# Splitting projection weights once instead of five times, and re-timing loads, operand splits and the last norm of an encoder-trunk kernel

## The chip, the core and the metric

The kernel runs on one core of a Trainium2 chip. The metric is the device time of one execution in microseconds (us), as a median of runs. The engines are named as in the profile: PE multiplies matrices, PEld loads PE's stationary operand beside it, DVE, ACT and POOL work elementwise, SP only issues DMA transfers, and 16 DMA engines carry them.

## What is computed

One layer on 2,304 tokens (2,048 of one sequence, 256 of another) of width 1,024, all in fp32: a norm, an input projection, three token mixers, an output projection with a residual, a norm, a gated feed-forward part with a width-3 convolution, a residual, and a last norm.

```python
h = rmsnorm(x, norm1_g)
q, k, v, g, lr, u, vs, xp = jnp.split(h @ w_in, IN_SPLITS, axis=-1)
a_out = gla_mixer(q, k, v, g, lr, gla_gate_w2, gla_gate_b, gla_norm_g)
b_out = spatial_gating(gelu(u), gelu(vs), sgu_ln_g, sgu_ln_b, sgu_w, sgu_b)
c_out = pool_mixer(xp, pool_w, pool_scale)
x = x + jnp.concatenate([a_out, b_out, c_out], axis=-1) @ w_o
a, up = jnp.split(rmsnorm(x, norm2_g) @ w_ffn_in, 2, axis=-1)
x = x + (silu(conv3(a)) * up) @ w_ffn_out
y = rmsnorm(x, norm_f)
```

## The kernel before, in words

**Products.** Every large product is made in a split form. `split` writes a high part of an fp32 operand (a copy on ACT into a rounded type) and a low part (a subtraction on DVE, or on POOL where it is asked to), and `mm3` multiplies high by high, high by low and low by high into one PSUM bank. So an operand costs one ACT and one DVE or POOL instruction before PE can use it.

**Stages.** A first sweep over 18 tiles of 128 tokens makes the attention part and prepares, beside it, the output projection's weights: `wo_prep(c)` loads column block c of eight, scales it, folds the pooling weights in and stores it to DRAM as `d_w[c]`. A second sweep goes over the tiles in five groups (`SUPERS`, of 3, 4, 3, 4 and 4 tiles); after each group `out2` multiplies its mixed tokens with all eight column blocks and adds the residual. The feed-forward part then goes over three blocks of 768 tokens, each as two halves q = 0 and 1. Per block, `ffn1` runs 22 times (j = 0 to 21): seven products of four steps, in a form with sums of operands (A and S are weight operands, B and T token operands). After every two or three of these, `ffn2` multiplies the result with eight column blocks of the second weight and adds it into `x2`. `finish` makes the last norm of a half, and `last_norm` that of the very last half.

**Order of the work.** PE's order is the order of the code. Beside it runs a `Pipe`: generators that issue a few instructions, then give a number of ticks to wait. `pipe.tick()` stands behind each step of three matmuls (about 0.53 us in the feed-forward part), so a number in a `yield` or in `pipe.add(gen, delay)` places elementwise work and DMAs beside a step of PE. From the second tile of the second sweep on, DVE, ACT, POOL and SP also keep the order of the code; in the first sweep a planner orders them. An instruction that waits holds all behind it on its engine, SP's DMAs too.

**Names that the change touches.** `wo_load` and `wo_split` load a half of `d_w[c]` (256 KB) and split it, in each of the five groups again; `ahead2` does the first ones before `out2` begins, and `look(u)` says how many column blocks ahead the loads go (2 in the last group, else 3). `xr_load` fetches the residual. `stat2` closes `out2`: short matmuls with one column each sum the squares. `load2f` fetches a half of `x2` (four DMAs for both halves); for the first block both are issued right after `out2`, ahead of the first `ffn1`. `bload` fetches the next block's token operands (16 pieces: four for each of four slices kk; pieces p = 0, 1, 2 hold two operands, p = 3 one) and splits them, from tick 30 of the block's last `ffn1` on, one piece each three ticks, in the order p = 0, 2, 1, 3; p = 1 and 3 have their low parts on POOL, p = 0 and 2 on DVE. It has one buffer per p, so a piece waits until PE has used the old one. `gate` makes the result of `ffn1`; the last gates of a block stand around ticks 21 to 31 of j = 21. In the last part `sqadd` squares each column of `x2` on ACT (two buffers) and adds it up on POOL. `prepw2` splits a piece of the second weight (`gh` on ACT, `gl` on DVE) six ticks before PE uses it.

In the tail, the rest of half 1's `finish` (products on DVE and output DMAs) is issued by `pipe.flush()` before `last_norm` begins:

```python
if final:
    pipe.flush()
    last_norm(blk, 0, xs, no, accs[0][0])
```

Of the kernel before, what the change touches and what calls it, by code (L numbers as in the profile page):

```python
# [10 lines left out]
F32 = mybir.dt.float32  # L11
# [7 lines left out]
P = 128  # L19
# [33 lines left out]
HL = (1, 2)  # L53
# [34 lines left out]
EARLY = 2  # L88
NAMES = ("A11", "S1", "S2", "S3", "S4", "A12", "A22")
# [31 lines left out]
def trunk(ctx: ExitStack, tc: tile.TileContext, xT, wa, wb, gw2, gb, rows, wsT, plw, wo, w1, w2, vec, cst, yT):  # L121
# [14 lines left out]
    def rawt(name):  # L136
        return rawp.tile([P, 1024], F32, tag="raw", name=name)
# [5 lines left out]
    d_w = [dr.tile([P, KD, P], F32, name=f"dw{c}") for c in range(KD)]  # L143
# [46 lines left out]
    if True:  # L190
# [273 lines left out]
        def wo_prep(c):  # L464
# [11 lines left out]
            GP.dma_start(out=d_w[c], in_=rv)  # L476
# [19 lines left out]
    if True:  # L496
# [163 lines left out]
        def wo_load(u, c, a):  # L660
            if u == len(SUPERS) - 1:
                rv = box2["acc"].tile([P, 4, P], F32, tag="wr", name="wr", bufs=4)
            else:
                if a == 0:
                    wx["raw", c] = rawt("rawo").rearrange("p (k n) -> p k n", k=KD)
                rv = wx["raw", c][:, 4 * a:4 * a + 4]
            wx["raw", c, a] = rv
            SY.dma_start(out=rv, in_=d_w[c][:, 4 * a:4 * a + 4])

        def wo_split(c, a):  # L670
            if a == 0:
                wx["h"] = box2["o"].tile([P, KD, P], F32R, tag="oh", name="oh")
                wx["l"] = box2["o"].tile([P, KD, P], F32R, tag="ol", name="ol")
            split(wx["h"][:, 4 * a:4 * a + 4], wx["l"][:, 4 * a:4 * a + 4], wx.pop(("raw", c, a)))
# [63 lines left out]
        def look(u):  # L738
            return 2 if u == len(SUPERS) - 1 else 3

        def ahead2(u):

            for c in range(look(u)):
                for a in range(2):
                    wo_load(u, c, a)
            wx[0] = xr_load(u, 0)
            yield 8
            for a in range(2):
                wo_split(0, a)
                wo_load(u, look(u), a)  # L750
                yield 2

        def out2(u, get, between=None, begun=None):
# [15 lines left out]
            for c in range(KD):  # L769
                oh, ol, xr = wx.pop("h"), wx.pop("l"), wx.pop(c)  # L770
                pw_ = pmt("pw") if c or not begun else begun
                for k in range(KD):
                    if c or not begun or k < 4:
                        mm3(pw_[:, 0:n], oh[:, k], ol[:, k], mh[:, k, 0:n], ml[:, k, 0:n], k == 0 and (c > 0 or not begun),
                            k == (3 if begun and not c else KD - 1))
# [92 lines left out]
    if True:  # L868
# [144 lines left out]
        def bload(bi, box):  # L1013
# [8 lines left out]

            for p, _ in PAIRS:
                load(0, p)
# [436 lines left out]
```

## Time and profile before

| what | value |
|---|---|
| median of 3 runs (lowest to highest) | 2462.21 us (2461.95 to 2464.28) |
| the profiled execution's own time | 2461.97 us |
| its span, first to last instruction | 2460.2 us |
| busy: PE | 2396.1 us, 97% |
| busy: DVE / ACT / POOL | 1655.8 / 1035.6 / 793.2 us |
| mean clock granted to PE | 0.989 of full |
| DMA | 343.52 MB, 140 GB/s mean |

The span lies 1.8 us below the time of its execution. Busy shares are means over stages that differ, so the text reads single stages. A clock of 1.00 is the level of 2.4 GHz, 0.50 that of 1.2 GHz; a window's figure between them is a mean over both.

### The profile page before, as it was taken

What the parts mean: (1) busy time and instruction counts of PE and PEld (TensorE: products, weight loads), DVE (VectorE), ACT (ScalarE), POOL (GpSimd) and SP (SyncE); (2) the same over time, 40 slices, a digit from 0 to 9 for tenths busy, and PEclk for the clock granted to TensorE, in tenths of its full rate; (3) what the DMA queues carried; (4) which work ended last, traced back from release to release, by engine and by line L of the source; (5) the groups of instructions that cost most, each with busy time, mean ns of one, the idle gap of its engine ahead of it and who ended that gap; (6) DMA issues with size and microseconds to landing.
All of it is one profiled execution on the core that took longest, in us unless ns stands there. A gap on an engine that the chain in (4) does not pass through costs nothing.

```text
span 2460.2 us, 37106 instructions
## 1 busy us (share of the span) xinstructions
PE 2396.1 (97%) x13416; PEld 2282.8 (93%) x13416; DVE 1655.8 (67%) x2963; ACT 1035.6 (42%) x1928; POOL 793.2 (32%) x748
## 2 busy tenths in 40 slices
PE   8999998999999989999999999999999999999997
PEld 7999997988988789999999899999999999999997
DVE  6755557676666876777867786666676665666666
ACT  6444444333332443433434544433344533444334
POOL 3332221010011664455545622323224521222122
PEclk9999999999999999999999999999999999999998
DMA  6333224555663653445434563444434543333232
GB/s 201 136 129 111 78 73 133 175 184 150 212 195 117 206 189 109 154 160 163 161 112 134 167 223 117 142 135 127 127 101 156 175 140 100 103 112 104 90 95 87
DMA packets 227772, 343.52 MB, mean 140 GB/s; under 512 B 25634, under 2 KB 124962, under 8 KB 227588
## 3 DMA queue, kind: packets, MB, share of 16 engines
q1 hardware_dynamic: 220564, 318.21, 41.2%
q0 software_dynamic: 6752, 22.55, 2.4%
q8 instruction: 106, 1.74, 0.3%
q14 instruction: 78, 0.64, 0.1%
q10 hardware_dynamic: 272, 0.39, 0.0%
HBM read 261.81 MB, written 79.25 MB: 139 GB/s over the span
## 4 chain that ended last, share of the span: by engine, by line
PE 52%; DVE 5%; issue 3%; POOL 3%; DMA 1%; ACT 1%; SPq 0%; DVEq 0%; POOLq 0%; ACTq 0%
PE py L172 7%; PE py L171 6%; PE py L170 6%; PE fA L1142 3%; PE fD L1140 3%; PE fA L1140 3%; PE fA L1141 3%; PE fD L1141 3%; PE fD L1142 3%; PE fB L1140 2%; PE fB L1142 2%; PE fB L1141 2%; PE fC L1140 2%; PE fC L1142 2%; PE fC L1141 2%
## 5 line engine op out<-in xcount | busy, mean ns | idle before, releaser
L163 POOL TENSOR_TENSOR S<-S,S 128x512 fp32r<-128x512 f32 x242 | 329.8, 1363 | 756.0 <-ACT S L162 719.3
L172 PE MATMUL py<-uh,gl 128*128 128x384 f32 (+1 forms) x1056 | 359.5, 340 | 6.3 <-DVE gl L1207 6.1
L170 PE MATMUL py<-uh,gh 128*128 128x384 f32 (+1 forms) x1056 | 359.8, 341 | 5.5 <-ACT gh L1205 5.4
L171 PE MATMUL py<-ul,gh 128*128 128x384 f32 (+1 forms) x1056 | 358.8, 340 | 3.8 <-DVE ul L1170 3.8
L1252 DVE TENSOR_TENSOR x<-py,x 128x384 f32<-128x384 f32 (+1 forms) x384 | 212.9, 556 | 159.4 <-PE py L172 157.5
L163 DVE TENSOR_TENSOR A<-A,A 128x512 fp32r<-128x512 f32 x198 | 157.0, 793 | 176.4 <-ACT A L162 167.9
L162 ACT ACTIVATE A<-A 128x512 fp32r<-128x512 f32 x198 | 124.4, 630 | 215.8 <-issue 71.3
L172 PEld LDWEIGHTS py<-uh,gl 128*128 128x128 f32 x1056 | 200.2, 190 | 10.0 <-DVE gl L1207 9.9
L162 ACT ACTIVATE S<-S 128x512 fp32r<-128x512 f32 x242 | 152.2, 629 | 135.3 <-PE fE L1142 63.9
L170 PEld LDWEIGHTS py<-uh,gh 128*128 128x128 f32 x1056 | 200.2, 190 | 7.8 <-ACT gh L1205 7.0
L171 PEld LDWEIGHTS py<-ul,gh 128*128 128x128 f32 x1056 | 200.0, 189 | 5.7 <-DVE ul L1170 5.3
L1205 ACT ACTIVATE gh<-rg 128x384 fp32r<-128x384 f32 (+1 forms) x198 | 97.3, 493 | 223.9 <-PE py L171 207.2
L1140 PE MATMUL fA<-B,A 128*128 128x386 f32 (+1 forms) x528 | 179.9, 341 | 0.0
L1142 PE MATMUL fA<-B,A 128*128 128x386 f32 (+1 forms) x528 | 179.1, 339 | 0.0
L1141 PE MATMUL fA<-B,A 128*128 128x386 f32 (+1 forms) x528 | 178.4, 338 | 0.0
L170 PE MATMUL pm<-wk,xh 128*128 128x512 f32 (+2 forms) x432 | 166.4, 385 | 7.3 <-ACT wk L165 7.3
L172 PE MATMUL pm<-wk,xl 128*128 128x512 f32 (+2 forms) x432 | 156.2, 362 | 1.3 <-DVE xl L163 1.3
L171 PE MATMUL pm<-wk,xh 128*128 128x512 f32 (+2 forms) x432 | 157.0, 363 | 0.1
L1207 DVE TENSOR_TENSOR gl<-rg,gh 128x384 fp32r<-128x384 f32 (+1 forms) x198 | 118.8, 600 | 11.6 <-ACT gh L1205 11.5
L170 PE MATMUL qm<-vk,xh 128*128 128x512 f32 x288 | 120.8, 420 | 2.0 <-ACT vk L165 2.0
L172 PE MATMUL pw<-mh,ol 128*128 128x512 f32 (+1 forms) x320 | 118.6, 371 | 3.0 <-DVE ol L163 3.0
L171 PE MATMUL pw<-ml,oh 128*128 128x512 f32 (+1 forms) x320 | 118.4, 370 | 0.0
(278 smaller groups left out, 6231.3 us busy)
## 6 DMA issues: line engine op xcount, KB each, us to landing
A<-in_w SPq DMA_DIRECT2D x242, 256.0 KB, 3.7
S<-ds_S SPq DMA_DIRECT2D x176, 256.0 KB, 2.7
rg<-in_w SPq DMA_DIRECT2D x150, 192.0 KB, 2.8
xt<-in_xT SPq DMA_DIRECT2D x35, 512.0 KB, 4.2
ds_S<-S SPq DMA_DIRECT2D x66, 256.0 KB, 2.3
rawo<-dw SPq DMA_DIRECT2D x64, 256.0 KB, 4.5
dx<-xr SPq DMA_DIRECT2D x24, 256.0 KB, 2.5
rg<-in_w SPq DMA_DIRECT2D x48, 128.0 KB, 2.4
```

The source lines that it names most:

```text
L162: SC.activation(hi, src, AF.Copy)
L163: (eng or V).tensor_tensor(out=lo, in0=src, in1=hi.bitcast(F32), op=ALU.subtract)
L170: TE.matmul(out, lh, rhs_h, start=first, stop=False)
L171: TE.matmul(out, lh, rhs_l, start=False, stop=False)
L172: TE.matmul(out, ll, rhs_h, start=False, stop=last)
L1140: TE.matmul(o, ah, bh, start=st, stop=False, skip_group_check=True)
L1141: TE.matmul(o, ah, bl, start=False, stop=False, skip_group_check=True)
L1142: TE.matmul(o, al, bh, start=False, stop=kk == 3, skip_group_check=True)
L1205: SC.activation(gh[:, 0:n], rv, AF.Copy)
L1207: V.tensor_tensor(out=gl[:, 0:n], in0=rv, in1=gh[:, 0:n].bitcast(F32), op=ALU.subtract)
L1252: V.tensor_tensor(out=x2[:, c, 1:1 + no], in0=py[q][:, 0:no], in1=x2[:, c, 1:1 + no], op=ALU.add)
```

## The change

The change has five parts, all in `trunk`. `wo_prep` splits its weights right after it has folded them and stores both parts (`d_w` becomes twice as large); `wo_load` fetches both parts of a half (512 KB) and `wo_split` is gone; all groups look three column blocks ahead, and the residual's first load goes ahead of the weights'. `bload` follows a written list `BORDER` of (kk, p, tick): the four pieces p = 2 at ticks 13 to 22 of the last `ffn1`, p = 0 and 1 at ticks 42 to 68, p = 3 at ticks 78 to 90; three loads go ahead instead of four. The first block's two `x2` loads are issued at ticks 30 and 60 of it. `stat2` after the last group comes at 16 ticks instead of 8, and `finish` of a non-final block starts at 14 and 36 ticks instead of 2 and 28. In the tail, `last_norm` is issued ahead of the rest of half 1's `finish`, which is flushed in its middle, and all its small diagonal pieces are made on ACT.

```diff
@@ -50,7 +50,9 @@
-HL = (1, 2)
+XG = 30
+BORDER = ((0, 2, 13), (1, 2, 16), (2, 2, 19), (3, 2, 22), (0, 0, 42), (0, 1, 45), (1, 0, 48), (1, 1, 52),
+          (2, 0, 56), (2, 1, 60), (3, 0, 64), (3, 1, 68), (0, 3, 78), (1, 3, 82), (2, 3, 86), (3, 3, 90))
@@ -86,6 +88,7 @@
+LOOK = 3
@@ -133,14 +136,14 @@
-    def rawt(name):
-        return rawp.tile([P, 1024], F32, tag="raw", name=name)
+    def rawt(name, dtype=F32):
+        return rawp.tile([P, 1024], dtype, tag="raw", name=name)
...
-    d_w = [dr.tile([P, KD, P], F32, name=f"dw{c}") for c in range(KD)]
+    d_w = [dr.tile([P, 2, KD, P], F32, name=f"dw{c}") for c in range(KD)]
@@ -473,7 +476,12 @@
             SC.activation(raw[:, 6 * P:8 * P], pf[:, 0:2 * P], AF.Copy)
-            GP.dma_start(out=d_w[c], in_=rv)
+            yield 2
+            hi = rawt("rawh", F32R)
+            split(hi, raw.bitcast(F32R), raw)
+            yield 3
+            GP.dma_start(out=d_w[c][:, 0], in_=hi.bitcast(F32).rearrange("p (k n) -> p k n", k=KD))
+            GP.dma_start(out=d_w[c][:, 1], in_=rv)
@@ -657,21 +665,9 @@
-        def wo_load(u, c, a):
-            if u == len(SUPERS) - 1:
-                rv = box2["acc"].tile([P, 4, P], F32, tag="wr", name="wr", bufs=4)
-            else:
-                if a == 0:
-                    wx["raw", c] = rawt("rawo").rearrange("p (k n) -> p k n", k=KD)
-                rv = wx["raw", c][:, 4 * a:4 * a + 4]
-            wx["raw", c, a] = rv
-            SY.dma_start(out=rv, in_=d_w[c][:, 4 * a:4 * a + 4])
-        def wo_split(c, a):
-            if a == 0:
-                wx["h"] = box2["o"].tile([P, KD, P], F32R, tag="oh", name="oh")
-                wx["l"] = box2["o"].tile([P, KD, P], F32R, tag="ol", name="ol")
-            split(wx["h"][:, 4 * a:4 * a + 4], wx["l"][:, 4 * a:4 * a + 4], wx.pop(("raw", c, a)))
+        def wo_load(c, a):
+            wx[c, a] = t = box2["o"].tile([P, 2, 4, P], F32R, tag="ow", name="ow", bufs=2 * LOOK)
+            SY.dma_start(out=t.bitcast(F32), in_=d_w[c][:, :, 4 * a:4 * a + 4])
@@ -735,20 +731,13 @@
-        def look(u):
-            return 2 if u == len(SUPERS) - 1 else 3
         def ahead2(u):
...
-            for c in range(look(u)):
+            wx[0] = xr_load(u, 0)
+            for c in range(LOOK):
...
-                    wo_load(u, c, a)
-            wx[0] = xr_load(u, 0)
-            yield 8
-            for a in range(2):
-                wo_split(0, a)
-                wo_load(u, look(u), a)
-                yield 2
+                    wo_load(c, a)
+                yield 1
...
         def out2(u, get, between=None, begun=None):
@@ -767,16 +756,16 @@
-                oh, ol, xr = wx.pop("h"), wx.pop("l"), wx.pop(c)
+                ow, xr = [wx.pop((c, a)) for a in range(2)], wx.pop(c)
...
                 for k in range(KD):
...
-                        mm3(pw_[:, 0:n], oh[:, k], ol[:, k], mh[:, k, 0:n], ml[:, k, 0:n], k == 0 and (c > 0 or not begun),
-                            k == (3 if begun and not c else KD - 1))
-                    if c + 1 < KD and k in (0, 1):
-                        wo_split(c + 1, k)
-                    if c + 1 + look(u) < KD and k in (3, 5):
-                        wo_load(u, c + 1 + look(u), k // 2 - 1)
+                        mm3(pw_[:, 0:n], ow[k // 4][:, 0, k % 4], ow[k // 4][:, 1, k % 4], mh[:, k, 0:n], ml[:, k, 0:n],
+                            k == 0 and (c > 0 or not begun), k == (3 if begun and not c else KD - 1))
+                    if k == 5 and c + LOOK < KD:
+                        wo_load(c + LOOK, 0)
+                    if k == 1 and 0 < c <= KD - LOOK:
+                        wo_load(c + LOOK - 1, 1)
@@ -790,7 +779,7 @@
-            pipe.add(stat2(u, acc, alloc), 8)
+            pipe.add(stat2(u, acc, alloc), 16 if between else 8)
@@ -854,7 +843,7 @@
-            mm3(begun[:, 0:w], wx["h"][:, k], wx["l"][:, k], mh[:, k, 0:w], ml[:, k, 0:w], k == 6, False)
+            mm3(begun[:, 0:w], wx[0, 1][:, 0, k % 4], wx[0, 1][:, 1, k % 4], mh[:, k, 0:w], ml[:, k, 0:w], k == 6, False)
@@ -924,7 +913,6 @@
-        PAIRS = ((0, V), (2, V), (1, GP), (3, GP))
@@ -1020,19 +1008,23 @@
-            for p, _ in PAIRS:
-                load(0, p)
-            yield box["wait"]
-            for kk in range(4):
-                for p, eng in PAIRS:
-                    m = 2 if p < 3 else 1
-                    hi, src = B[p][:, 0, 0:m, kk, 0:w], got.pop((kk, p))
-                    SC.activation(hi, src, AF.Copy)
-                    yield HL[0]
-                    eng.tensor_tensor(out=B[p][:, 1, 0:m, kk, 0:w], in0=src, in1=hi.bitcast(F32), op=ALU.subtract)
-                    yield HL[1]
-                    if kk < 3:
-                        load(kk + 1, p)
+            todo = [(kk, p) for kk, p, _ in BORDER]
+            for kk, p in todo[:NX - 1]:
+                load(kk, p)
+            at = 0
+            for n, (kk, p, tick) in enumerate(BORDER):
+                if tick > at:
+                    yield tick - at
+                    at = tick
+                m = 2 if p < 3 else 1
+                hi, src = B[p][:, 0, 0:m, kk, 0:w], got.pop((kk, p))
+                SC.activation(hi, src, AF.Copy)
+                yield 1
+                (GP if p % 2 else V).tensor_tensor(out=B[p][:, 1, 0:m, kk, 0:w], in0=src, in1=hi.bitcast(F32), op=ALU.subtract)
+                yield 1
+                at += 2
+                if n + NX - 1 < len(todo):
+                    load(*todo[n + NX - 1])
@@ -1319,11 +1311,8 @@
-                o, i, sc = dg[:, b * P:b * P + n], ident[:, P - n:P], r[:, b:b + 1]
-                if b % 2:
-                    SC.activation(o, i, AF.Copy, scale=sc)
-                else:
-                    V.tensor_scalar(out=o, in0=i, scalar1=sc, scalar2=None, op0=ALU.mult)
+                SC.activation(dg[:, b * P:b * P + n], ident[:, P - n:P], AF.Copy, scale=r[:, b:b + 1])
+            pipe.flush()
             TE.matmul(pr, ones, dg, start=True, stop=True)
@@ -1343,13 +1332,20 @@
-        xs = {q: load2f(segs, q, box["w"]) for q, segs in enumerate(BLOCKS[0])}
+        xs = {}
+        def first_x(w):
+            for q, segs in enumerate(BLOCKS[0]):
+                xs[q] = load2f(segs, q, w)
+                yield XG
+        pipe.add(first_x(box["w"]), XG)
...
-            nbox = {"wait": 30}
+            nbox = {}
@@ -1374,14 +1370,13 @@
             if final:
-                pipe.flush()
...
                         nx[q] = load2f(segs, q, w)
-                    pipe.add(finish(blk, q, xs, no, accs[q][0], FG, nxt), 2 + 26 * q)
+                    pipe.add(finish(blk, q, xs, no, accs[q][0], FG, nxt), 14 + 22 * q)
...
```

## Rows read from the trace of the kernel before

**Rows 1.** The page, section 1: busy time, share of the span, instructions.
```profile
PE 2396.1 (97%) x13416; PEld 2282.8 (93%) x13416; DVE 1655.8 (67%) x2963; ACT 1035.6 (42%) x1928; POOL 793.2 (32%) x748
```

**Rows 2.** The view of waits, PE alone: us in total, times, longest.
```profile
PE pw L172 <- DVE ol L163: 3.0, 3, 2.0
```

**Rows 3.** PE's timeline: start, us, instruction; in brackets the idle time before it.
```profile
854.40 1.19 PE L688 MATMUL pn<-ones,acc 128*128 128x1 f32 x8 [1.69 <-DVE acc L767]
...
871.66 0.66 PE L1140 MATMUL fD<-B,A 128*128 128x386 f32 x1 [6.11 <-DVE u L1149]
...
1364.31 0.44 PE L171 MATMUL py<-ul,gh 128*128 128x384 f32 x1 [2.06 <-DVE ul L1170]
...
1383.61 0.44 PE L170 MATMUL py<-uh,gh 128*128 128x384 f32 x1 [2.14 <-ACT gh L1205]
...
1384.98 0.69 PE L172 MATMUL py<-uh,gl 128*128 128x384 f32 x1 [0.76 <-DVE gl L1207]
...
1399.25 0.83 PE L1272 MATMUL pn<-ones,acc 128*128 128x1 f32 x6 [1.06 <-POOL acc L1226]
...
1907.92 0.44 PE L170 MATMUL py<-uh,gh 128*128 128x384 f32 x1 [2.13 <-ACT gh L1205]
...
1924.07 1.44 PE L1272 MATMUL pn<-ones,acc 128*128 128x1 f32 x6 [2.75 <-POOL acc L1226]
```

**Rows 4.** Windows behind six waits: us, busy (count) by engine, PEclk, DMA share, GB/s.
```profile
826.50:832.00 5.50, 5.12 (x15) 3.61 (x16) 5.50 (x7) 1.47 (x4) 3.11 (x3) 0.69 0.69 228
854.40:859.00 4.60, 4.60 (x20) 4.60 (x21) 0.77 (x2) 1.75 (x4) 3.56 (x3) 0.63 0.94 311
871.66:876.50 4.84, 4.84 (x17) 4.84 (x18) 3.15 (x4) 3.83 (x5) 4.76 (x4) 0.59 0.39 144
1383.60:1392.00 8.40, 7.64 (x26) 7.32 (x27) 6.41 (x8) 5.86 (x11) 8.40 (x7) 0.59 0.62 186
1907.90:1914.00 6.10, 5.33 (x20) 5.01 (x21) 4.46 (x7) 4.49 (x8) 6.10 (x5) 0.72 0.47 149
1924.07:1932.00 7.93, 7.93 (x31) 7.93 (x32) 1.88 (x4) 1.51 (x4) 2.94 (x3) 0.61 0.21 67
```

**Rows 5.** Groups by line, shapes kept apart: busy us, mean ns, idle before.
```profile
L1226 POOL TENSOR_TENSOR acc<-acc,sq 128x384 f32<-128x384 f32 x28 | 36.6, 1325 | 0.0
...
L163 DVE TENSOR_TENSOR ol<-wr,oh 128x512 fp32r<-128x512 f32 x16 | 13.4, 870 | 0.0
```

**Rows 6.** Windows of the two sweeps, columns as in rows 4.
```profile
123.00:369.00 246.00, 245.91 (x1573) 225.98 (x1572) 140.06 (x298) 116.92 (x219) 69.83 (x134) 1.00 0.27 98
441.00:848.00 407.00, 403.63 (x2032) 347.09 (x2031) 275.40 (x624) 145.63 (x285) 72.74 (x66) 1.00 0.58 179
614.30:654.30 40.00, 40.00 (x223) 38.39 (x222) 27.07 (x59) 16.85 (x35) 2.62 (x2) 1.00 0.72 234
799.50:848.00 48.50, 45.49 (x189) 35.50 (x189) 43.60 (x55) 24.57 (x54) 31.34 (x27) 0.96 0.71 218
```

**Rows 7.** SP's timeline behind the second sweep.
```profile
853.71 7.00 SPq L906 DMA_DIRECT2D x<-dx  x4
```

**Rows 8.** The chain that ended last, in that stretch: start, us, what.
```profile
861.45 8.15 DMA A<-in_w
```

**Rows 9.** Line 1032: duration in ns (min/median/max), first and last start.
```profile
L1032 DVE TENSOR_TENSOR B<-b,B x16: 952/1308/1598, 1365.1 to 1914.4; 128x772 fp32r<-128x772 f32 x8, 128x776 fp32r<-128x776 f32 x8
...
L1032 POOL TENSOR_TENSOR B<-b,B x16: 1012/1802/2182, 1367.9 to 1921.6; 128x772 fp32r<-128x772 f32 x4, 128x386 fp32r<-128x386 f32 x4, 128x776 fp32r<-128x776 f32 x4, 128x388 fp32r<-128x388 f32 x4
```

**Rows 10.** Windows of the last `ffn1` of blocks 0 and 1, columns as in rows 4.
```profile
1344.80:1359.50 14.70, 14.70 (x86) 14.70 (x85) 12.54 (x18) 7.95 (x15) 6.20 (x5) 1.00 0.99 333
1870.00:1884.80 14.80, 14.80 (x86) 14.80 (x85) 10.78 (x19) 7.83 (x16) 4.21 (x4) 1.00 0.75 257
```

**Rows 11.** DMA issues: count, KB each, median us to landing.
```profile
b<-db SPq DMA_DIRECT2D x12, 386.0 KB, 3.7
```

**Rows 12.** DVE's timeline in the tail.
```profile
2443.34 3.27 DVE L1289 SCALAR_TENSOR_TENSOR x<-x,vc,acc 128x386 f32<-128x386 f32 x6
```

## Prediction, made before the change was run

> **What bounds the kernel now.** I read the page first: PE is busy for 2396.1 us [rows 1], so of the 2460.2 us of span only 64 are to be had, and they stand where PE waits. The view of waits, filtered to PE, then says for whom, and PE's timeline says when: the reader is to look at the bracket at the end of each line, the idle time before it and its releaser. The waits come in four places. In the last group's `out2` (799 to 848 us) PE waits 3.0 us for `ol`, the low part of a projection weight [rows 2]. Just behind it come 1.69 us before `stat2`'s short matmuls and 6.11 us for a DVE addition [rows 3]. At the ends of blocks 0 and 1 come, in order, a wait for `ul` (2.06 us at the first end), a pair for `gh` and `gl` (2.14 and 0.76; the second end has the like, from 2.13) and one for POOL's `acc` (1.06 and 2.75) [rows 3]. Last comes the tail. Third, I looked at the granted clock right behind each wait, in windows that begin when PE resumes. It lies between 0.59 and 0.72 there [rows 4], so PE pays twice: the wait, and (1 - clock) of the window. That is 1.7, 1.7, 2.0, 3.4, 1.7 and 3.1 us, 13.6 in all.
>
> **The clock.** The rows say that a wait or a close pair of 2.9 us and more is followed by the low level, that 2.75 was too, and that 2.06 alone was not: PE ran at 1.00 after it. The 1.69 us fell together with eight one-column matmuls and was followed by 0.63 [rows 3, 4].
>
> **Weights split once.** Removed are 80 pairs of ACT and DVE instructions, 16 for each group; in the last group those on DVE take 870 ns each, 13.4 us [rows 5]. In the groups before PE has no wait (40.00 of 40.00 us busy in the third [rows 6]), so nothing is gained there. In the last one DVE is busy for 43.6 of 48.5 us [rows 6], the splits are most of 13.4 of these, and PE's wait for them goes: 3.0 us and the 1.7 of clock behind it, 4.7. The bounds are 0 (the same wait comes back for the weights' DMA) and 4.7; I take 4.7, because loads three of eight column blocks ahead have some 18 of these 48.5 us to land. The price is eight splits of twice the width and eight more stores in the first sweep. By twice the nearest row they are below 8 x 1.74 = 14 us of DVE, over a stretch in which DVE is busy 140 of 246 us and PE never waits [rows 6]: cover enough, so nothing. If that cover were gone, the 14 us would be paid. SP has two weight buffers instead of four to run ahead with, and the token loads queue behind it. Since these loads have the same sweep as cover, I put them at nothing too.
>
> The other price is traffic. Eighty loads grow by 256 KB, 21.0 MB. In the tightest group 234 GB/s took a share of 0.72, so a full share is 325 GB/s, and 21.0 MB are 64.5 us of transfer. From 441 to 848 us the DMA engines are free for 0.42 x 407 = 171 us [rows 6]. It is hidden if the loads can use that; in the tightest group 11.2 us are free in 40 and 12.9 are wanted, of which the first three column blocks are fetched before. Nothing is lost in my sum; the bound is a rival.
>
> **`stat2` later.** The 1.69 us wait is for the last sum of squares, which eight more ticks (4.2 us) cover. The eight short matmuls stay, so I take the wait and half the clock behind it: 2.5 (bounds 1.7 and 3.4).
>
> **`x2` loads later.** SP spends 7.00 us on the four loads [rows 7], and the weight load issued behind them lands 8.15 us after its issue [rows 8]. ACT, then DVE stand waiting for it, and PE's 6.11 us are what is left when the slack is used up; with 2.0 of clock that is 8.1. At ticks 30 and 60 two halves go out instead of all, each behind most of the next `ffn1`'s loads: of the four only the last is queued behind it, and it has 12 ticks, 6.3 us. Half of SP's 7.0 plus half of the 8.15 is 7.6, so each half may still hold DVE for about 1 us. I take 8.1 - 2 = 6 (bounds 0 and 8.1). `x2` is needed only from tick 113 on.
>
> **The ends of blocks.** Behind the `ul` wait stand at the first end 2.14 + 0.76 + 1.06 and 3.4 of clock, 7.4; at the second 2.13 + 0.76 (as at the first) + 2.75 and 1.7 + 3.1 of clock, 10.4. The cause is POOL: `gh` stands behind a square on ACT, which waits for one of two buffers, which POOL's sums free. POOL has 14 sums of 1.33 us [rows 5] to do in 42 ticks of 0.53, 22 us, and between them eight low parts, p = 1 at 1.8 and p = 3 from 1.0 us [rows 9]. That is 18.6 + 11.2 = 29.8 us or more. The change puts p = 3 behind the block's end, which leaves 25.8, still above 22. So the `acc` wait goes (`finish` also starts 12 ticks later), and the pair shrinks: I leave 1.3 us of it at each end, between 0 and 2.9. That frees 17.8 - 2.6 = 15.2.
>
> But four pieces p = 2 now go into the last `ffn1`, three ahead of its first gate. Each takes 0.95 to 1.6 us of DVE, 1.3 at the median [rows 9], so 3.9 us stand ahead of the gate, where DVE is idle for 2.2 us at the first end and 4.0 at the second [rows 10]. And the fourth piece is only issued after the first is split, some 7 ticks or 3.7 us before its own, while such a load lands 3.7 us after issue at the median [rows 11], with the DMA engines at 0.99 in the first end's stretch [rows 10]. A load that is late there holds ACT, and behind it the gates, whose products PE waits for already. I let the `ul` wait grow by 3 us at the first end and 1.5 at the second (bounds 0, and 3.9 plus 3.7), and let the clock fall behind the first fully (2 us, the x2 case) and behind the second half the time (1). That costs 7.5, and the ends together give 7.7.
>
> What the low parts cost where POOL is at work is seen in the spread from 0.95 to 1.6 us [rows 9]. The Trainium skill, SBUF — State Buffer, section "Who interferes with whom", says that DVE with two SBUF inputs and a POOL instruction that reads SBUF lock each other out for a whole instruction. By that rule the three pieces could each stand behind a POOL split and cost 3 us more than I took at each end, some 6 us together; that would bring out the second rival below.
>
> **The tail.** Six products of half 1, 3.27 us, stand on DVE in front of the last norm's two small instructions [rows 12]. They now run while POOL and ACT work on the chain; but the diagonal, made on two engines before, is made on one, and the products must be done before the last multiplications all the same. I take 0.8 (bounds 0 and 3.3).
>
> **The sum.** 4.7 + 2.5 + 6 + 7.7 + 0.8 = 21.7, from the profiled execution's 2461.97: 2440.3, so 2440. That execution is 0.24 us below the median of the runs, which I leave out. All upper ends together (4.7 + 3.4 + 8.1 + 17.8 + 3.3 = 37) would give 2425.
>
> **Rivals.** *The gates pay for the splits* (0.24): at both ends the `ul` wait grows as much as the later waits shrink. For it speaks that DVE has 2.2 idle us where 3.9 are put, against it the 4.0 of the second end. Without the 7.7 the time is 2448. *The `x2` loads collide again* (0.10): each half delays weight loads so that PE waits as before, in two pieces; against it speaks the halved queue. Without the 6 the time is 2446. *The change doesn't do what it says* (0.09): in the last group PE waits for the weights' DMA in place of `ol` (the share there is 0.71 already [rows 6], and some 2.6 MB come on top, 8 us of 48), the ends give nothing, and only `stat2` and the tail are left: 2459. *Slower, by traffic* (0.07): the loads are tied to PE's pace, and of the 64.5 us of added transfer too little finds a free moment. It decides when more than 27 us of it show as waits of PE for the weights in the second sweep; with half of it showing, 32, the time is 2440 + 32 = 2472. Against it speaks that free DMA time is 2.6 times what is wanted.
>
> **How the numbers follow.** My forecast holds 0.50, with its own range from 2430 to 2447. What a measurement can tell from no change is 0.2%, 5 us. The forecast and the first two rivals are faster, 0.84; the third counts as no change, 0.09; the last is slower, 0.07. The range goes from 2428 (the forecast's terms near their upper ends) to 2456, which takes in the first two rivals with a block end that loses some, and leaves out the last two and a little below.
>
> **What would show it.** Right, if PE's view of waits has no wait for weights in `out2`, the 6.11 us and the waits for `acc` are gone, the second sweep still has none, and the `gh` waits at the block ends shrink. The step on the gates is right if the `ul` waits at the ends grow beyond 2.06 us. The prediction is wrong if the first sweep, ordered by the planner, shows new waits, if weights land late in the groups of three tiles, or if POOL, still holding p = 3, is late for the next block's first products.

## The result: slower, and the profile after

The changed kernel takes 2475.75 us (median of 4 runs, 2473.52 to 2478.32) against 2462.08 us (4 runs, 2461.94 to 2464.28) for the kernel before on the same chip. The ratio is 1.0052, with a 95% interval from 1.0040 to 1.0064. The prediction was 2440 us, faster; the time lies outside its range, on the side of its last rival.

To find the place, I read the starts of PE's instructions in the timeline of both traces and took differences between fixed points: first product of the second sweep (`qm`), first `ffn1` of each block (`fA`), and first product of the first and last `ffn2` of each block (`py`). In the changed kernel the second sweep goes from the first of these rows to the second:

```profile
379.28 0.51 PE L173 MATMUL qm<-vk,xh 128*128 128x512 f32 x1 [0.86 <-ACT vk L168]
...
866.92 0.34 PE L1132 MATMUL fA<-B,A 128*128 128x386 f32 x1
```

| stretch of PE's time | before, us | after, us | difference |
|---|---|---|---|
| first sweep | 379.41 | 379.28 | -0.1 |
| second sweep | 468.88 | 487.64 | **+18.8** |
| block 0: first `ffn1` to first `ffn2` | 75.16 | 68.62 | **-6.5** |
| block 0 and 1: ends, and the starts of blocks 1 and 2 | 197.66 | 197.69 | 0.0 |
| middles of the three blocks | 1293.05 | 1293.76 | +0.7 |
| tail | 46.04 | 46.01 | 0.0 |

These make 12.8 us, which is the difference of the spans (2473.0 and 2460.2). PE does the same work as before [rows 1], and waits more:

```profile
PE   2397.1 (97%) x13416; PEld 2278.0 (92%) x13416; DVE 1618.5 (65%) x2889; ACT 999.3 (40%) x1858; POOL 785.5 (32%) x756
...
DMA packets 239163, 368.68 MB, mean 149 GB/s; under 512 B 25762, under 2 KB 125090, under 8 KB 238980
```

PE's view of waits (us in total, times, longest) names new releasers where `ol` stood [rows 2]: the transfers of weights, of the pooling part `mh`, and the residual `xr`.

```profile
PE py L175 <- DVE gl L1199: 9.2, 10, 1.6
PE pw L173 <- DMA ow<-dw: 7.9, 4, 2.6
PE fD L1132 <- DVE u L1141: 6.2, 5, 2.6
PE pw L173 <- DMA mh<-dc: 4.7, 2, 2.5
PE py L174 <- DVE ul L1162: 4.4, 3, 2.1
PE pw L173 <- DVE xr L774: 2.2, 3, 1.0
```

PE's timeline says when. The waits for `mh` are in groups 1 and 2, those for `xr` in group 3, those for `ow` in groups 3 to 5:

```profile
456.52 0.44 PE L173 MATMUL pw<-mh,ow 128*128 128x384 f32 x1 [2.15 <-DMA mh<-dc]
550.80 0.47 PE L173 MATMUL pw<-mh,ow 128*128 128x512 f32 x1 [2.50 <-DMA mh<-dc]
637.13 0.41 PE L173 MATMUL pw<-mh,ow 128*128 128x384 f32 x1 [1.35 <-issue]
656.92 0.45 PE L173 MATMUL pw<-mh,ow 128*128 128x384 f32 x1 [0.93 <-DVE xr L774]
660.72 0.44 PE L173 MATMUL pw<-mh,ow 128*128 128x384 f32 x1 [1.44 <-DMA ow<-dw]
735.31 0.47 PE L173 MATMUL pw<-mh,ow 128*128 128x512 f32 x1 [2.60 <-DMA ow<-dw]
864.07 0.50 PE L173 MATMUL pw<-mh,ow 128*128 128x512 f32 x1 [2.15 <-DMA ow<-dw]
```

SP's timeline shows why `mh` is late. Six weight loads, 3 MB, are issued in one go ahead of it:

```profile
442.48 0.39 SPq L676 DMA_DIRECT2D xr<-in_xT  x1
442.91 4.48 SPq L670 DMA_DIRECT2D ow<-dw  x6
447.45 0.67 SPq L634 DMA_DIRECT2D mh<-dc  x1
```

In the view of DMA issues from 436 to 460 us (count, KB each, median us to landing) these 128 KB take 9.0 us to land:

```profile
ow<-dw SPq DMA_DIRECT2D x8, 512.0 KB, 8.1
...
mh<-dc SPq DMA_DIRECT2D x1, 128.0 KB, 9.0
```

At the block ends [rows 3] the pair for `gh` and `gl` shrank and the waits for `acc` are gone, but others stand there: `uh` and `ul` together 3.3 and 2.7 us, a further wait for `gl` 5 us behind the pair (1.37 and 1.36 us), and a wait for `u` at the start of the next block (1.37 and 2.64 us). Of the first end, and the last wait of the second:

```profile
1375.01 0.44 PE L173 MATMUL py<-uh,gh 128*128 128x384 f32 x1 [1.24 <-ACT uh L1160]
1377.51 0.44 PE L174 MATMUL py<-ul,gh 128*128 128x384 f32 x1 [2.06 <-DVE ul L1162]
1396.61 0.45 PE L173 MATMUL py<-uh,gh 128*128 128x384 f32 x1 [0.51 <-ACT gh L1197]
1397.99 0.44 PE L175 MATMUL py<-uh,gl 128*128 128x384 f32 x1 [0.75 <-DVE gl L1199]
1402.77 0.45 PE L175 MATMUL py<-uh,gl 128*128 128x384 f32 x1 [1.37 <-DVE gl L1199]
...
1994.20 0.66 PE L1132 MATMUL fD<-B,A 128*128 128x388 f32 x1 [2.64 <-DVE u L1141]
```

### The profile page after: what moved, and what is told of

Read it like the earlier page. It is cut to its first block, busy times and chain, and to the rows that moved or that the text cites. A ratio compares the mean times of both kernels' runs of the same rounds, so it can differ in the third digit from the quotient of the medians.

```text
span 2473.0 us, 36941 instructions
## 1 busy us (share of the span) xinstructions
PE 2397.1 (97%) x13416; PEld 2278.0 (92%) x13416; DVE 1618.5 (65%) x2889; ACT 999.3 (40%) x1858; POOL 785.5 (32%) x756
## 4 chain that ended last, share of the span: by engine, by line
PE 68%; DMA 9%; DVE 8%; issue 4%; POOL 3%; ACT 2%; SPq 1%; DVEq 0%; POOLq 0%; ACTq 0%
PE py L175 6%; PE py L174 6%; PE py L173 6%; PE pm L173 3%; PE pm L174 3%; PE pm L175 3%; PE fA L1134 3%; PE fA L1132 3%; PE fA L1133 3%; PE fD L1132 2%; PE fD L1133 2%; PE fD L1134 2%; DMA A<-in_w 2%; DMA dx<-xr 2%; PE qm L173 2%
## 5 line engine op out<-in xcount | busy, mean ns | idle before, releaser
L166 DVE TENSOR_TENSOR A<-A,A 128x512 fp32r<-128x512 f32 x198 | 163.1, 824 | 171.9 <-ACT A L165 154.5
L173 PE MATMUL pw<-mh,ow 128*128 128x512 f32 (+1 forms) x320 | 119.6, 374 | 16.2 <-DMA ow<-dw 7.9
L567 POOL TENSOR_TENSOR so<-so,mhalf 128x4 f32<-128x4 f32 x18 | 18.5, 1028 | 318.7 <-DVE so L565 318.7
```

Source lines behind the costliest of these rows:

```text
L166: (eng or V).tensor_tensor(out=lo, in0=src, in1=hi.bitcast(F32), op=ALU.subtract)
L173: TE.matmul(out, lh, rhs_h, start=first, stop=False)
L567: GP.tensor_tensor(out=so, in0=so, in1=mhalf[:, 0:4], op=ALU.pow)
```

## The experiments

Each ratio is against the kernel before, run on the same chip in the same rounds, with its 95% interval. Stage times come from one profile each. Such a stage can differ by itself: from the second sweep's first product to the first `pw` the kernels took 69.8 to 72.7 us, with no relation to their edits. So a stage difference below 3 us proves little alone.

### The two halves of the change

The change was cut in two. `e1_split_alone`: the kernel before with only the weights split once (`wo_prep`, `wo_load`, `ahead2`, `out2`).

> Only the weights' part of the change, on the kernel before: split once in the first sweep, both parts loaded (512 KB a half), three column blocks ahead in all groups; all other parts undone. If the whole loss comes from this part, the second sweep (first product to first ffn1) takes 487.6 us as in the changed kernel instead of 468.9, and the time is about 2462 + 19 = 2481. If the loss comes from elsewhere (the planner's order in the first sweep, or the other parts), it stays within 5 us of 2462.

`e2_rest_alone`: the kernel before with all the rest.

> The opposite: all parts but the weights' one, on the kernel before. If the parts add up, the second sweep is that of before (468.9 us with its wait for the split weights), the first ffn1 to the first ffn2 takes 68.6 instead of 75.2, and the time is 2475.8 - 18.8 = 2457. If the other parts lived from the freed DVE, the gain in front of the first ffn2 is smaller and the time is 2462 or more.

Measured: e1 2482.96 us, ratio 1.0075 (1.0059 to 1.0092); e2 2458.66 us, 0.9979 (0.9970 to 0.9989). The second sweep took 492.04 us in e1 and 469.52 in e2. The whole loss belongs to the weights' part; the rest is a gain, of 5 us instead of the 17 that were predicted for it.

### What the second sweep waits for

`e3_mixer_first`: the changed kernel, with each group's last `mh` and `ml` loads ahead of the weights' in SP's queue.

```diff
-pipe.add(pool2(i, get, t0), hold(6))
+last = seq[n + 1][0] != seq[n][0]
+pipe.add(pool2(i, get, t0), hold(2 if last else 6))
```

> The changed kernel, but the pooling part's two small loads (mh, ml, 128 KB each) of each group's last tile are issued four ticks earlier, ahead of the group's first six weight loads instead of behind them. Theory order (small loads stand in the queue behind 3 MB of weights): the wait in the first column block goes in groups one to three (2.15, 2.50 and 1.35 us, with some clock behind them), so about 6 to 9 us less, 2468. Theory traffic (the bytes do not fit): the same time is lost a column block later, in waits for the weights, and the time stays within 3 us of 2476.

`e4_four_xr`: the changed kernel with four residual buffers instead of two in groups 1 to 4.

```diff
+if u < len(SUPERS) - 1:
+    xr = rawt("xr")[:, 0:512].rearrange("p (a t) -> p a t", a=4)
```

> The changed kernel, but the residual's loads of groups one to four have four buffers instead of two (from the pool that held the raw weights). Theory loop (a residual load waits for the store of two column blocks before, and load plus store take longer under the doubled traffic): the groups of three tiles, 37.6 and 40.2 us, get shorter by 2 to 5 us each, and the time is 2468 to 2472. Theory traffic: the waits become waits for weights, the groups stay as long, and the time stays within 3 us of 2476.

Measured: e3 2469.74 us, 1.0027 (1.0017 to 1.0036), second sweep 479.05 us; e4 2473.82 us, 1.0044 (1.0029 to 1.0059), second sweep 485.53. The order of a few loads is worth 8.6 us of the sweep (487.64 to 479.05): groups 1, 2, 4 and 5 are back at 33.12, 43.65, 43.34 and 50.94 us between first and last product, and `mh` lands in 2.7 us. The residual's buffers are worth next to nothing.

What is left in e3 against the kernel before stands in group 3, 41.32 us against 33.12. SP's timeline shows a queue that stands for 8.4 us, because the store of normalised rows `dh` waits for a load `hh` that was issued behind the six weight loads. The residual loads behind it are late, and PE's row gives the wait:

```profile
616.65 4.91 SPq L671 DMA_DIRECT2D ow<-dw  x6
621.61 1.20 SPq L719 DMA_DIRECT2D hh<-dx  x2
631.25 0.32 SPq L724 DMA_DIRECT2D dh<-hh  x1
...
632.25 0.59 SPq L677 DMA_DIRECT2D xr<-in_xT  x1
...
640.18 0.44 PE L173 MATMUL pw<-mh,ow 128*128 128x384 f32 x1 [3.29 <-DVE xr L775]
```

`e5_spread`: e3 with `yield 5` for `yield 1` between the weight loads in `ahead2`.

> e3_mixer_first with the six weight loads ahead of a group issued five ticks apart in pairs instead of one after the other. Of e3's 10.2 us of loss in the second sweep 8.2 stand in the third group alone (41.32 us against 33.12), where SP holds a store of the normalised rows for 8.4 us, because the load that it waits for stands behind 3 MB of weights. If the order in SP's one queue is the cause, the third group returns to 33 to 36 us and the time is 2461 to 2464. If it is the traffic itself (the third group alone moves normalised rows too), the bytes are the same, the group stays above 39 us, and the time is 2468 to 2471.

`e11_pool_queue`: e3 with the `hh` loads and `d_h` stores issued by POOL.

```diff
-SY.dma_start(out=h[c], in_=d_x[u][:, c, o:o + w])
+GP.dma_start(out=h[c], in_=d_x[u][:, c, o:o + w])
```

> e3_mixer_first with the loads and stores of the normalised rows (hh, d_h) issued from POOL's queue instead of SP's; the bytes are the same. If SP, standing 8.4 us at a store of these rows, holds back the weight and residual loads behind it, the third group falls from 41.32 us to 35 to 38, and the time is 2464 to 2467, no lower, since the DMA engines are at a share of 0.9 to 0.99 there once nothing is held back. If the bytes alone set it, the group stays at 41 us and the time at 2469 to 2470.

Measured: e5 2466.55 us, 1.0011 (1.0001 to 1.0020), group 3 37.72 us; e11 2467.65 us, 1.0012 (1.0003 to 1.0021), group 3 39.24 us. e5 lies between the two theories: group 3 recovers 3.6 of its 8.2 us. e11 recovers 2.1, less than its expectation had, and its second sweep (480.89 us) is no shorter than that of e3; whether the other queue gained anything is open. Windows of group 3 (length, then busy time of PE, PEld, DVE, ACT, POOL; at the end granted clock, DMA share, GB/s) show what bounds the group in e5: the DMA engines are at a share of 0.90 to 0.99 for 32 us. In the first two windows PE lives on what has been fetched, in the next three it waits.

```profile
623.00:631.00 8.00, 8.00 (x47) 7.84 (x46) 2.60 (x6) 0.51 (x2) 0.00 (x0) 1.00 0.99 348
631.00:639.00 8.00, 8.00 (x48) 8.00 (x47) 1.67 (x4) 0.84 (x3) 0.00 (x0) 1.00 0.90 266
639.00:647.00 8.00, 7.04 (x40) 6.40 (x39) 3.05 (x7) 1.19 (x4) 0.00 (x0) 1.00 0.95 316
647.00:655.00 8.00, 6.71 (x37) 6.07 (x37) 1.97 (x5) 1.00 (x3) 0.00 (x0) 1.00 0.99 324
655.00:663.00 8.00, 7.09 (x42) 6.63 (x41) 3.34 (x8) 2.04 (x6) 0.00 (x0) 1.00 0.69 218
```

### The bytes

`e10_half`: e3 with half of each weight load.

```diff
-t = box2["o"].tile([P, 2, 4, P], F32R, tag="ow", ...)
-SY.dma_start(..., in_=d_w[c][:, :, 4 * a:4 * a + 4])
+t = box2["o"].tile([P, 1, 4, P], F32R, tag="ow", ...)
+SY.dma_start(..., in_=d_w[c][:, 0:1, 4 * a:4 * a + 4])
```

> e3_mixer_first with half of each weight load: only the high parts are fetched, and the products that would read the low parts read the high ones (the low parts of the projection weights are left out; the number of products is the same). If what is left of the loss in the second sweep is the added transfer, in the queue or on the DMA engines, the third group returns to 33 us, the second sweep to 468 to 470 us, and the time is 2459 to 2461. If the loss comes from the new order of the residual loads or from the tiles' buffers, which stay, it remains at 2467 to 2470.

`e15_after_half`: the same edit on the changed kernel itself.

> The changed kernel with half of each weight load: only the high parts are fetched, and the products that would read the low parts read the high ones (the low parts of the projection weights are left out). Order in SP's queue as in the changed kernel. If the order costs only because six loads of 512 KB stand there, the waits for mh go, the second sweep is 463 to 465 us as in e10_half, and the time is 2450 to 2455. If mh stands behind any weight loads too long, the waits of 2.15 and 2.50 us stay in part, the sweep is 467 to 472, and the time is 2456 to 2461.

Measured: e10 2456.55 us, 0.9970 (0.9957 to 0.9982); e15 2455.30 us, 0.9970 (0.9960 to 0.9981). With half the bytes every group is at its time of before or below: 33.11, 43.60, 33.11, 43.34 and 45.59 us in e10, and 33.11, 43.60, 33.32, 43.34 and 45.92 in e15. PE has no wait for `mh` or `xr` in either, and in the same stretch of group 3 all windows of e10 are full:

```profile
631.00:639.00 8.00, 8.00 (x48) 8.00 (x47) 2.66 (x7) 1.46 (x4) 0.00 (x0) 1.00 0.82 257
639.00:647.00 8.00, 8.00 (x48) 8.00 (x48) 3.34 (x8) 1.45 (x4) 0.00 (x0) 1.00 0.78 254
```

In e15 `mh` stands behind six loads too, and lands in 6.9 us, which is early enough. So the order costs only because of the doubled bytes. The second sweep is 463.58 us in e10, 5.3 below the kernel before and all of it in the last group (45.59 us against 50.94): that is what splitting once gives where its transfer is free. In e15 the sweep is 466.05 us, 1 above its expectation; most of the difference from e10 stands ahead of the first `pw` (72.1 us against 70.4). Against e10 the five groups of the changed kernel lose 4.5, 2.9, 7.1, 3.1 and 4.0 us, the third, which had the least free DMA time, the most. e10 came below its expectation (2459 to 2461), because I had left this gain out.

`e8_last_only`: the change, with groups 1 to 4 fetching a third, unsplit copy and splitting it as before.

```diff
+if u == len(SUPERS) - 1:
+    SY.dma_start(out=owt(c, a).bitcast(F32), in_=d_w[c][:, 0:2, 4 * a:4 * a + 4])
+    return
+SY.dma_start(out=rv, in_=d_w[c][:, 2, 4 * a:4 * a + 4])   # split later
```

> The whole change, but only the last group reads the split weights; the four groups before it read the unsplit ones (a third copy, written in the first sweep) and split them as before. If the loss is the added transfer in the groups of three and four tiles, the second sweep is as before in these groups, the last group loses its waits for ol, and the time is 2455 to 2457, some 2 us below e2_rest_alone (2458.66). If the splits and stores in the first sweep cost something, or the weights' transfer in the last group does, it is 2459 or more.

Measured: 2457.74 us, 0.9977 (0.9968 to 0.9987), no different from e2 by its interval, and between the two cases of its expectation. Groups 1 to 4 are as before; in the last one two waits for `ow` (1.47 and 1.51 us) stand where three for `ol` were. This was the prediction's third rival in small.

### The ends of blocks

e2 with one edit undone: `e6_old_pieces` keeps the later `finish` and puts the old order of the pieces back; `e7_old_finish` keeps `BORDER` and puts the old ticks back. `e12_front_only` has neither edit.

```diff
-pipe.add(finish(blk, q, xs, no, accs[q][0], FG, nxt), 14 + 22 * q)
+pipe.add(finish(blk, q, xs, no, accs[q][0], FG, nxt), 2 + 26 * q)
```

> e2_rest_alone with the pieces of the token operands in their old order (all four kinds of a column block in turn, from 30 ticks on), and the sums of squares still started 12 ticks later. If the early p = 2 pieces hold the gates, the waits for uh and ul at the block ends go back from 3.3 to 2.1 us and from 2.7 to 1.4, the waits behind them stay as small as they are, and the time is 2455 to 2457. If the new order is what keeps POOL free for the sums, the waits for gh, gl and acc come back (2 to 4 us at each end), and the time is 2460 to 2463.

> e2_rest_alone with the sums of squares and the x2 loads behind a block at their old ticks (2 and 28 instead of 14 and 36), and the pieces in the new order. If the late second x2 load is what delays the first gate weights of the next block, PE's waits for u there (1.4 and 2.6 us in the changed kernel) go, and with the clock behind them the time is 2453 to 2456. If the later start is what keeps PE from waiting for acc at the end, that wait (1.06 and 2.75 us before) comes back, and the time is 2459 to 2462.

> The kernel before with only the later stat2, the spread first x2 loads and the last norm's order: neither the weights' part, nor the new order of the pieces, nor the later sums behind a block. e7_old_finish (new order alone on top of this) gave 2452.74, e6_old_pieces (later sums alone on top) 2454.61, both 2458.66. If each of the two removes the wait for acc and the pair for gh and gl by itself, and only together do they cost, this is 2457 to 2459. If the new order gains nothing by itself, it is 2452 to 2454.

| kernel | pieces | `finish` | ratio (95%) | ends and next starts, us |
|---|---|---|---|---|
| e12 | old | old | 0.9985 (0.9976 to 0.9994) | 201.3 |
| e6 | old | later | 0.9964 (0.9951 to 0.9977) | 193.4 |
| e7 | new | old | 0.9958 (0.9944 to 0.9972) | 193.1 |
| e2 | new | later | 0.9979 (0.9970 to 0.9989) | 197.3 |

Each edit alone gains against e12. Both together gain less than either, though by the ratios alone this is weak (e2's interval overlaps with both); the stretch says it too: it took 195.9 to 199.4 us in the nine kernels with both edits, and 197.7 to 201.3 in the three with neither. e12 came above its expectation (2457 to 2459) with 2460.66. The rows tell why. Between the points of the stretch, PE's idle time in the timeline is 16.9, 13.4, 11.4 and 15.2 us (e12, e6, e7, e2), and the time at a clock of 0.50 costs 7.7, 3.1, 4.7 and 4.8 more; what is left is 177 us in all four. In e12 PE waits 4.26 and 4.30 us for `acc`, POOL's sums; this is the longest wait, and each edit alone removes it:

```profile
1395.21 1.44 PE L1276 MATMUL pn<-ones,acc 128*128 128x1 f32 x6 [4.26 <-POOL acc L1230]
```

But each brings a wait of its own, and both together bring both. The later `finish` also moves the next `x2` load, which in e2 goes out right ahead of the next block's first weights `rg`; PE then waits for `u` (1.73 and 1.97 us, and 2.21 and 1.93 in e6). With the old ticks (e7) that wait is not there. In the changed kernel the same chain reads, in order of time, first in SP's timeline and then in the chain that ended last:

```profile
1977.98 0.40 SPq L1286 DMA_DIRECT2D out_y<-x  x1
...
1983.15 1.24 SPq L895 DMA_DIRECT2D x<-dx  x2
...
1986.17 1.00 SPq L1190 DMA_DIRECT2D rg<-in_w  x2
```

```profile
1977.98 5.10 DMA out_y<-x
...
1986.17 6.27 DMA rg<-in_w
...
1992.47 0.53 ACT gh L1197
...
1993.50 0.57 DVE u L1141
...
1994.20 0.66 PE fD L1132
```

The `x2` load goes out just after the store `out_y` of the norm's result has landed, and `rg` stands behind it in SP's queue. The `rg` load takes 6.27 us there, against a median of 2.8 in the page, but it takes 6.7 and 7.0 us in e7 too: a slower load is not the reason. It goes out too late. In e7 it is issued 11.9 and 11.8 us ahead of the next block's first `ffn2`; in e2 it is 10.6 and 10.5, and 1.73 and 1.97 of these are the wait itself. The new order, on the other hand, brings the waits for `uh` (1.4 and 0.7 us in e7) and the further wait for `gl` (1.35 and 1.37), which e6 doesn't have.

The next three try to keep only what gains. `e9_best` is e8 with the old ticks of `finish`, and with p = 2 back behind the gates:

```diff
+BORDER = tuple((kk, p, t + 12 * kk) for kk in range(4) for p, t in ((0, 30), (2, 33), (1, 37))) + tuple(
+    (kk, 3, 78 + 4 * kk) for kk in range(4))
```

> A version meant to keep what gained: e8_last_only (split weights read by the last group alone) with the sums of squares and x2 loads behind a block at their old ticks, and the pieces p = 0, 2, 1 of each column block from tick 30 on, only p = 3 behind the block's end. e7_old_finish without the weights' part gave 2452.74. If the early p = 2 pieces cost the waits for uh (1.42 and 0.67 us) and the acc wait stays away because p = 3 is late, this is 2448 to 2451. If POOL needs the early order too, acc is late again and it is 2453 to 2456.

`e13_later_pn` moves the first half's `finish` six ticks later and leaves the `x2` loads at their ticks (by a shorter `yield` ahead of the first of them, not shown); `e14_old_weights` is e13 with the weights' path of the kernel before.

```diff
-pipe.add(finish(blk, q, xs, no, accs[q][0], FG, nxt), 2 + 26 * q)
+pipe.add(finish(blk, q, xs, no, accs[q][0], FG, nxt), 8 + 20 * q)
```

> e9_best with the sums over partitions of the first half six ticks (3.2 us of PE) later at the ends of blocks 0 and 1; the x2 loads stay at their ticks. If the 3.29 us for which PE waits for acc at each end are only a matter of when the short matmuls stand in its order, both waits go with the clock behind them, and the time falls from 2452.3 to 2443 to 2447. If POOL's chain of sums is the bound there, the wait moves to the next thing that needs it, and it is 2450 to 2453.

> e13_later_pn with the projection weights as in the kernel before (fetched unsplit and split in every group). If the split weights in the last group are worth what the waits for ol cost (4 us with the clock), this is 3 to 5 us slower than e13_later_pn; if their own waits for the weights' DMA (1.5 to 3.5 us in e8 and e9) take that back, the two are within 1.5 us.

Measured: e9 2452.28 us, 0.9950 (0.9938 to 0.9963); e13 2450.90, 0.9954 (0.9940 to 0.9967); e14 2453.22, 0.9959 (0.9947 to 0.9972). All three beat the kernel before and the changed one, and cannot be told from each other or from e7. e9 lies between the two cases of its expectation. In e9 the waits for `uh` and `gh` are gone, and `acc` is waited for again:

```profile
1376.91 0.45 PE L175 MATMUL py<-uh,gl 128*128 128x384 f32 x1 [0.25 <-DVE gl L1228]
1390.78 0.83 PE L1293 MATMUL pn<-ones,acc 128*128 128x1 f32 x6 [3.29 <-POOL acc L1247]
```

e13 removes that wait, and gains nothing: PE waits for `u` in the next block instead (1.27 and 1.37 us behind the first end, 0.64 behind the second, and there 1.84 for POOL's `S`). The ends and next starts are 190.3 us in e9 and 192.3 in e13. The expectation that only the tick was wrong fell; its rival, that the wait moves on, stands. Whether split weights are worth anything in the last group is not settled: e13 and e14 are within each other's intervals, and the group took 48.69, 52.27 and 51.88 us in e8, e9 and e13.

## Why the prediction was wrong

| term | predicted, us | measured, us |
|---|---|---|
| splits gone | -4.7 | -5.3 (e10) |
| traffic of the weights | 0 | +24.1 |
| `stat2` and `x2` loads | -8.5 | -6.5 |
| ends of blocks | -7.7 | 0.0 |
| tail | -0.8 | 0.0 |

**The step that failed** is "It is hidden if the loads can use that", with "Nothing is lost in my sum". The traffic's measured cost is the changed kernel's second sweep less e10's, 487.64 - 463.58 (less e15's, it is 21.6); 17.9 us of it are idle time of PE. The order in the queue makes 8.6 of it and goes away with e3; 15.5 remain with that order and go away with half the bytes. My sum held 64.5 us of transfer against 171 us of free DMA time in the whole sweep, a mean over stretches that differ. Its own figures for the third group said otherwise: 11.2 us free in 40, and 12.9 wanted. I excused the difference with the three column blocks that are fetched before the group. But these do a part of the harm: 3 MB in one go, just ahead of the small loads that PE needs first. The larger part is left when the small loads go first: of the 15.5 us, 8.2 stand in the third group (41.32 us in e3 against 33.11), where the residual loads are late, and 5.4 in the last (50.94 against 45.59), where PE waits for the weights themselves. The step on the first sweep, whose splits and stores I put at nothing, held: 379.28 us against 379.41.

The Trainium skill, DMA: Bandwidth & Descriptors, section "Two DMAs through the same engine are not ordered", says that within one queue of one DMA engine, descriptors start in order. The trace agrees with that: `mh` landed 9.0 us after its issue behind six loads, and 2.7 ahead of them.

**The rival came, with its price.** "Slower, by traffic" wanted more than 27 us of waits in the second sweep, and gave 2472. 24 us were enough, since the other terms gave 6.5 instead of the 17 of the sum. It had a chance of 0.07 because the argument against it was the mean.

**The ends of blocks.** What the prediction wanted to remove was removed: the waits for `acc` (3.8 us) went, the pair for `gh` and `gl` shrank from 2.9 us to 1.26 and 1.22 (I had left 1.3 each), and the clock behind them stayed at 1.00 (8.2 us). That is 15.3 us, where the sum had 15.2. The early pieces p = 2 cost the gates something, as it said: `uh` and `ul` together grew by 1.2 us at the first end and by 1.4 at the second, against 3 and 1.5, and the clock fell behind both, 1.7 us each, against 2 and 1. What failed is that the sum had nothing for waits that come in place of the removed ones. The further wait for `gl` (1.37 and 1.36) comes with the new order, and what delays that piece was not tried. The wait for `u` (1.37 and 2.64, with 1.4 of clock behind the second) comes because `finish` carries the next `x2` load with it, and I costed only its sums. That load is the collision that I had priced for the first block and not looked for here. Together these are 8 us, and the 7.7 of the sum are gone. Nor are single waits there independent: in e12 the `gh` wait of the first end is 1.2 us shorter than before and the one for `acc` 3.2 longer, and the short matmuls come 40.2 us after the last `ffn2` began, as they did before (39.8).

**The lock.** The prediction feared up to 3 us at each end for pieces on DVE that meet a POOL instruction. Of the four p = 2 pieces at the first end three took 0.96 us, and the third, which met one, 1.86:

```profile
1368.04 0.96 DVE L1023 TENSOR_TENSOR B<-b,B 128x772 fp32r<-128x772 f32 x1
1369.38 1.86 DVE L1023 TENSOR_TENSOR B<-b,B 128x772 fp32r<-128x772 f32 x1
```

```profile
1369.13 1.30 POOL L166 TENSOR_TENSOR S<-S,S 128x512 fp32r<-128x512 f32 x1 [6.09 <-ACT S L165]
```

The DVE row ends 0.81 us after the POOL row does, about as if it had begun when that ended. At the second end it is again the third piece, 2.00 us beside the others' 0.96, and it ends 0.82 us after a POOL row that had begun ahead of it. So the rule of the Trainium skill, SBUF — State Buffer, section "Who interferes with whom", fits these rows. But it met one piece of four, not three, and cost 0.9 and 1.0 us. The prediction tied this cost to its second rival, the `x2` loads; by its cause it belongs to the first, the gates.

**The first block and the tail.** Of PE's timeline in the changed kernel, a wait for POOL's `S` and one for `u` in the first block, and the one behind the last norm's chain:

```profile
906.62 0.45 PE L1134 MATMUL fD<-B,S 128*128 128x386 f32 x1 [0.74 <-POOL S L166]
...
933.36 0.41 PE L1132 MATMUL fD<-B,A 128*128 128x386 f32 x1 [1.79 <-DVE u L1141]
...
2460.87 1.66 PE L1316 MATMUL pr<-acc,ones 128*128 128x386 f32 x2 [2.85 <-ACT acc L1314]
```

The waits of 1.69 and 6.11 us [rows 3] are gone, and so is the low clock behind them. The 1.79 us for `u` are no remainder of the 6.11; the kernel before has the same wait at the same place, 2.2 us ahead of the first `ffn2`:

```profile
921.26 0.41 PE L1140 MATMUL fD<-B,A 128*128 128x386 f32 x1 [1.81 <-DVE u L1149]
```

What is new are five waits for POOL's `S`, 2.8 us together. Every kernel with the later `x2` loads and `stat2` has four to seven of them, and the two without these edits (before, e1) have none; the sum had nothing for them. The 6.5 us are one profile: in the fourteen other kernels with these edits the stretch took 68.4 to 72.0 us, a gain of 3 to 7. In the tail the wait for the chain was 3.63 us before; it is 0.8 us shorter, and the end came no earlier. What took the 0.8 us back there was not tried.

**The clock.** The prediction read from the rows that a wait of 2.9 us and more is followed by the low level and one of 2.06 is not. Its own rows hold a case against that, the 2.0 us for `ol` with a window at 0.69 behind it [rows 2, 4]. In the changed kernel 2.15 us for `mh` (456.52) were followed by a window at 0.69, and 2.50 us (550.80) and 2.60 us (735.31) by windows at 1.00. So the length of a wait alone did not tell what the clock does behind it.

## What to carry to other kernels

Weigh added transfer against the free DMA time of the tightest stretch and against the moments at which it is issued, not against the free time of a whole sweep; what stands behind the burst in the same queue pays for it. Splitting an operand once instead of each time trades engine time for bytes: here it could pay only where that engine was waited for, in one group of five. And two edits that remove the same wait don't add, while the waits that each brings do; of a step that is moved, look first at the loads that it takes along.

## What was not expected of the hardware

A load of 128 KB landed after 2.7, 6.9 or 9.0 us with nothing of its size changed, by whether none, 1.5 MB or 3 MB of weights stood ahead of it in the queue (e3, e15 and the changed kernel). In 8 us windows of group 3 a DMA share of 0.98 to 1.02 meant 324 to 358 GB/s (e5 and e11), close to the 325 that I had worked out for a full share from the trace of before.
